# Query and key rows of two heads rounded in one step and moved to their tiles by transfers on chip, with a new order of the queues

## The chip, the cores and the metric

The kernel runs on one core of a Trainium2 chip. The metric is device time in microseconds (us) of one execution. Engines are called as in the profile: PE (TensorE), with its weight loads as PEld, DVE (VectorE), ACT (ScalarE), POOL (GpSimd) and SP (SyncE), of which the last here only issues transfers (DMAs) from memory.

## What is computed

The reference is one decoder block for 512 tokens of width 1024: a recurrent branch (RG-LRU) and a branch of latent attention with 16 heads, merged by gates, then a convolved feed-forward part (FFN). The change lies in the attention branch. Cut to what matters:

```python
q = (rmsnorm(q_lat, q_norm_g[l]) @ w_uq[l]).reshape(B, S, H, QK_NOPE + QK_ROPE)   # 64 + 32
q_rope = rotary(q[..., QK_NOPE:], positions)
q = jnp.concatenate([q[..., :QK_NOPE], q_rope], axis=-1)
kv = (rmsnorm(kv_lat, kv_norm_g[l]) @ w_ukv[l]).reshape(B, S, H, QK_NOPE + V_HEAD)
k_nope, v = kv[..., :QK_NOPE], kv[..., QK_NOPE:]
k_r = jnp.broadcast_to(rotary(k_rope, positions)[:, :, None, :], (B, S, H, QK_ROPE))
k = jnp.concatenate([k_nope, k_r], axis=-1)
y_mla = causal_block_attention(q, k, v)
```

## The kernel before

Activations lie transposed: features on the 128 partitions, the 512 tokens along the row. Every matmul is done in float32r with each operand split into a rounded high part and the low rest (three matmuls instead of one, mm3, L255). A split is therefore always a pair: ACT rounds a copy (the high part), DVE subtracts it from the source (the low part). Weights are loaded by SP into "raw" buffers (L242) and split into "whl" or "whg" (L221 and L222).

The order in time is: latents and modulation of the first norm (0 to 60 us), attention (60 to 240), the recurrence (240 to 380), the two output projections (to 460), the norm and the FFN (to the end). In between stand matmuls of the gates ("fill", L544) and sums for the second modulation (L781 on DVE), which are independent of the attention and are put where something is waited for.

For the attention the 16 heads form four groups g. A head's query tile "q" and key tile "kt" have 96 rows in use: 64 without rotation ("nope") and 32 rotated ("rope"). q_nope(g, i), L671, projects the nope rows of two heads i at once: one 128x512 result in the PSUM bank "fil", rows 0 to 63 of the first head and 64 to 127 of the second. evac_half (L666) then splits 64 rows at a time straight into rows 0 to 63 of each head's tile: L668 on ACT and L669 on DVE, twice. k_nope(g, i), L688, does the same for two key tiles. There is one bank "fil"; the next projection into it waits until both halves have been read. q_rope(g), L679, rotates the rope rows of four heads in one tile "rp" (of which one buffer exists), and q_rope_put (L684) brings each head's 32 rows to rows 64 to 95 of its query tile by a DMA on chip, issued by POOL (L686). head_a (L715) computes scores (L725 to L727: high by high, high by low, low by high), softmax, and transposes the probabilities (L747); head_b (L753) multiplies by the values (L760).

The order in which each engine does its instructions up to the FFN is written out by hand: QUEUES (L103) has for each engine a table of numbers in base 36, the places that instructions have in the order of the code, and queue_order (called at L1068) chains them in the order of the table. So the order does not follow from the code alone.

Of the kernel before, what the change touches and what calls it, by code (L numbers as in the profile page):

```python
# [98 lines left out]
GACC = ()  # L99
ROOM = -1  # L100
# [4 lines left out]
        0-7 b 8 c 9 d a e-u w-x 1h-1i v 10 13 y 1j 16 19 1c z 1k 11 14 12 15 17-18 1a-1b 1d-1g 1l-21 26 29 2c 22  # L105
        2n-2q 27-28 2a 23 2b 24-25 2d-2h 38-3b 2i-2m 2r-37 3c-3f 3t 3g 3u-3v 3h 3w 3i-3s 3x 40 43 46 3y 41 44 47
        49-4a 3z 42 45 48 4b 4e 4h 4k 4n 4f 4i 4l 4c-4d 4o 4q-4r 4g 4j 4m 4p 4s-4v 5j-6i 7s-7t 6j 7u-80 6k-6u 7j-7q
        81-89 4w-53 7r 54-58 6v-6z 59 70 5a 8m 71 5b 72 8n-8r 5c 73 5d 74 91 94 9a 5e 75 9b 95-99 92-93 8s-90 9c 5f
        76-78 5g-5i 79-7h 9n-9y 7i ba bd-bk 9z-aa 9d 9h 9l 9i-9k 9e-9g 9m bb-bc bl aj-ao 8a-8c ab-ad cp cs cy ae-af
        8d-8h cz ct-cv bm bq-bt bn-bp cw-cx cq-cr d0 ag ap-ax bu-bv ea ed ej-ek ee-ei bw-bz eb-ec el ah-ai 8i-8l  # L110
        ay-b1 c4-cc d1-d4 c0-c3 d5-d8 b2-b4 dj-do b5 d9-da b6-b9 db-df cd-ch em-ep ci dp-ds eq-et dt-dx eu-ev dg-di
        fg fj-fq ew cj-cl ex fh ey-ez fi fr g2-gd hp-hs hy-hz ht-hx ge-gp i0 f0-f1 fs fw-fy f2 fz f3 ft-fv cm-co
        dy-e9 g0 gq gy-h3 gr-gt g1 f4-f6 j4 j7 jd gu j8-jb i1-i4 jc je j5-j6 jf i5-i8 h4-h5 i9-ia h6-ha ib-ie hb-hc
        if gv-gx kp ks ky-kz kt-kx ig-ii kq-kr l0 f7-fa ij-ir fb jg jk-jn jh-jj jo-jp fc-fd jy-k3 fe-ff hd-hg jq-js
        l1-l4 jt-ju hh-hn l5-la jv-jx ho k4-kc lb-li is-iu lj lm ls-lt ln-lr lk-ll lu iv-iw m5-m7 ng m8 nh-ni ix
        nj-nr m9-mg iy-j3 kd-ke mh-ms kf-kh lv-lz m3 m0-m2 m4 ki n1-n6 mt-n0 ns nw-nz nt-nv p7 pa-pf o0-o1 p8-p9
        n7-nf kj-kl pg r4-r6 km-ko ph-pi r7-ra oj-ol rd-re om rb on rc rf oo-op oa-oi oq-ox q1-q6 oy-p6 o2 pj-pm
        o3-o9 pn-pq sa sd sj-sk se-si pr-ps q7-qf ua-uc pt rg-rn pu-q0 sb-sc sl qg-qj ro-rp qk-ql sw qm sx-sy ud-ul
        sz rq t0-t7 rr-rx qn-qo sm-st qp t8-tj qq-qx ts-tx su-sv qy-r0 vg vj vp r1-r2 vk-vo vh-vi vq-vr r3 tk um
        uq-ut un wa-wc uo-up tl wd-wl tm uu-uv tn-tp uw-uz tq-tr ry v0 rz-s0 v1-v3 s1 vs-vv s2-s9 ty vw-vz tz w0-w1  # L120
        u0-u9 w2 wm-wp w3 wq-wt w4-w9 v4-v6 wu-wv v7-v8 ww-wy 104-107 v9 wz-x0 va x1-x2 vb x3 vc-vf x4-x7 xg-xh x8
        xi-xn x9 xo xa xp-xr xb-xe xs-xt xf xu-z6 108-109 z7-z8 10a-10t zg 10u zh 10v zi-zo 112-113 zp-zq 114-11d zr
        z9 10w 10y 110 10x 10z 111 11e-11p zs-101 11w-11x 102-103 11y-127 za-zd 128-129 ze-zf 12a-12j 11q-11r 11t
        11s 11u-11v 12q-136 13e-13f 137 13g-13p 148-149 12k-12l 12n 12m 12o-12p 14a-14c 13q-13r 14d-14f 13s-141
# [1397 lines left out]
```

## Time and profile before

| | us |
|---|---|
| median of 3 runs | 845.07 |
| lowest and highest of them | 843.25, 846.47 |
| the profiled execution | 844.61 |
| its span, first to last instruction | 842.8 |
| PE busy | 827.0 |
| DVE busy | 744.3 |
| ACT busy | 542.0 |
| POOL busy | 23.9 |

A row of the profile names the line of the code, the engine, the operation and the tiles (out<-in, without buffer numbers). In a table of groups there follow the shapes and the count, after the first bar the busy time in us and the mean ns of one, after the second bar the engine's idle time just before them and who ended it. In a timeline a row has the start in us and the time it took, and in brackets the idle time before it with its releaser. Matmuls overlap in PE's pipeline: one of 512 columns is shown with 0.4 us, but they start 0.23 us apart.

### The profile page before, as it was taken

How to read it: one execution, taken by the hardware profiler on the slowest of the kernel's cores; microseconds unless marked ns; L12 is line 12 of the kernel's file. 1: busy time of each engine (PE TensorE's matmuls, PEld its weight loads, DVE VectorE, ACT ScalarE, POOL GpSimd, SP SyncE). 2: the span in 40 equal slices, each digit the busy share in tenths (PEclk: the TensorE clock that was granted, in tenths of full speed). 3: DMA queues.
4: the chain of work that ended last, by engine and by line, in shares of the span. 5: the costliest groups of instructions: out<-in, count | busy, mean ns of one | idle time of the engine just before them, and what ended most of it. 6: DMA issues, size and time to landing. Idle time of an engine off the chain costs nothing. (4 is left out here: it accounts for less than half of the span.)

```text
span 842.8 us, 12809 instructions
## 1 busy us (share of the span) xinstructions
PE 827.0 (98%) x4612; PEld 697.8 (83%) x4612; DVE 744.3 (88%) x1440; ACT 542.0 (64%) x1032; POOL 23.9 (3%) x47
## 2 busy tenths in 40 slices
PE   7999999999999999999999999999999999999996
PEld 4777888888877777777877898899889889889985
DVE  7989898998957899998689769999999999999985
ACT  7585877777846888893145567676666666545533
POOL 0001000000020000000000001000000000000000
PEclk9999999999999999999999999999999999999999
DMA  9923233344573232227665155332232233522222
GB/s 348 376 93 86 85 104 125 103 151 119 173 177 96 75 111 87 97 89 276 210 234 192 74 187 137 88 115 94 93 115 95 90 117 135 194 73 101 103 99 100
DMA packets 35107, 114.15 MB, mean 135 GB/s; under 512 B 4434, under 2 KB 8146, under 8 KB 34532
## 3 DMA queue, kind: packets, MB, share of 16 engines
q1 hardware_dynamic: 32548, 107.01, 36.3%
q0 software_dynamic: 2496, 6.33, 3.7%
q8 instruction: 36, 0.59, 0.3%
q14 instruction: 27, 0.22, 0.1%
HBM read 106.47 MB, written 4.23 MB: 131 GB/s over the span
## 5 line engine op out<-in xcount | busy, mean ns | idle before, releaser
L221 ACT ACTIVATE whl<-raw 128x512 fp32r<-128x512 f32 (+2 forms) x149 | 84.4, 573 | 71.0 <-PE tr L260 25.4
L221 ACT ACTIVATE whg<-raw 128x512 fp32r<-128x512 f32 x136 | 84.6, 625 | 43.1 <-PE acc L260 9.8
L222 DVE TENSOR_TENSOR whg<-raw,whg 128x512 fp32r<-128x512 f32 x136 | 92.5, 686 | 14.0 <-ACT whg L221 13.2
L222 DVE TENSOR_TENSOR whl<-raw,whl 128x512 fp32r<-128x512 f32 (+2 forms) x149 | 91.3, 619 | 10.0 <-ACT whl L221 9.3
L737 ACT ACTIVATE P<-P,mx,qsc 128x512 f32<-128x512 f32 (+3 forms) x64 | 41.2, 647 | 7.7 <-DVE mx L733 7.7
L1199 DVE SCALAR_TENSOR_TENSOR Y<-acc,vec,Y 128x511 f32<-128x511 f32 (+1 forms) x38 | 28.2, 745 | 9.0 <-ACT Y L1197 8.8
L1199 DVE SCALAR_TENSOR_TENSOR Y<-Y,vec 128x511 f32<-128x511 f32 (+1 forms) x48 | 35.3, 746 | 0.4
L258 PE MATMUL gm<-A,whg 128*128 128x512 f32 x88 | 35.4, 402 | 0.0
L260 PE MATMUL gm<-A,whg 128*128 128x512 f32 x88 | 35.4, 402 | 0.0
L259 PE MATMUL gm<-A,whg 128*128 128x512 f32 x88 | 35.2, 400 | 0.0
L258 PE MATMUL tr<-A,whl 128*128 128x512 f32 x80 | 32.1, 402 | 0.0
L258 PE MATMUL acc<-A,whg 128*128 128x512 f32 x80 | 31.8, 397 | 0.0
L260 PE MATMUL tr<-A,whl 128*128 128x512 f32 x80 | 31.7, 397 | 0.0
L259 PE MATMUL tr<-A,whl 128*128 128x512 f32 x80 | 31.7, 396 | 0.0
L260 PE MATMUL acc<-A,whg 128*128 128x512 f32 x80 | 31.7, 396 | 0.0
L259 PE MATMUL acc<-A,whg 128*128 128x512 f32 x80 | 31.6, 395 | 0.0
L730 DVE CUSTOM_DVE_ANT_0 P<-acc,mr 128x256 f32<-128x256 f32 (+2 forms) x64 | 28.6, 486 | 2.1 <-PE acc L727 1.7
L221 ACT ACTIVATE pt<-tr 128x512 fp32r<-128x512 f32 (+1 forms) x48 | 23.5, 520 | 8.4 <-PE tr L747 6.5
L222 DVE TENSOR_TENSOR pt<-tr,pt 128x512 fp32r<-128x512 f32 (+1 forms) x48 | 27.6, 594 | 0.2
L760 PE MATMUL tr<-pt,v 128*128 128x384 f32 (+3 forms) x128 | 27.7, 324 | 0.0
L260 PE MATMUL acc<-A,whl 128*128 128x512 f32 x64 | 25.7, 401 | 0.0
L259 PE MATMUL acc<-A,whl 128*128 128x512 f32 x64 | 25.3, 395 | 0.0
(601 smaller groups left out, 2572.6 us busy)
## 6 DMA issues: line engine op xcount, KB each, us to landing
raw<-in_w_up SPq DMA_DIRECT2D x44, 512.0 KB, 3.5
raw<-in_w_dn SPq DMA_DIRECT2D x22, 512.0 KB, 3.5
wa<-in_w_adat SPq DMA_DIRECT2D x16, 512.0 KB, 9.5
raw<-in_w_adat SPq DMA_DIRECT2D x16, 512.0 KB, 3.3
raw<-in_w_xr SPq DMA_DIRECT2D x10, 512.0 KB, 3.5
raw<-in_w_pr SPq DMA_DIRECT2D x10, 512.0 KB, 4.1
raw<-in_w_gm SPq DMA_DIRECT2D x8, 512.0 KB, 4.2
raw<-in_w_gr SPq DMA_DIRECT2D x8, 512.0 KB, 3.5
```

The lines of the kernel that those rows point to most:

```text
L221: S.activation(h, src, AF.Copy)
L222: return V.tensor_tensor(dst[:, 1, lo_c:lo_c + n], src, h.bitcast(F32), SUB).ins
L258: PE.matmul(out, wh, x[:, 0, xs], start=start, stop=False)
L259: PE.matmul(out, wh, x[:, 1, xs], start=False, stop=False)
L260: return PE.matmul(out, wl, x[:, 0, xs], start=False, stop=stop).ins
L730: V.tensor_tensor_reduce(out=pt[:, POFF[qd]:POFF[qd] + n], in0=sc[qd], in1=mask[:, T - n:], scale=1.0, scalar=-3e38, op0=ADD, op1=ALU.max, ...
L737: S.activation(pq, pq, AF.Exp, scale=qsc[:, qb:qb + 1], bias=mx[:, qb:qb + 1], accum_out=sm[:, qb:qb + 1])
L760: PE.matmul(yb[:, kb * P:], vv, pth[:, part, off:off + n], start=(i == 0 and part == 0), stop=(i == 3 and part == 1))
L1199: V.scalar_tensor_tensor(u[:, d:], src[:, :T - d], vc("fw", (2 - d) * 2 * NF + cj), u[:, d:], MUL, ADD)
```

## The change

Three things are changed.

First, the query rows. The weight columns of w_q are swapped on the host, so that the second head of a pair comes out in rows 0 to 63 and the first in rows 64 to 127. The new evac splits all 128 rows in one pair of steps into the second head's tile. The first head's rows, which then lie in rows 64 to 127 of the wrong tile, are brought to rows 0 to 63 of their own tile by a DMA on POOL's queue (move). The put of the second head's rope rows writes rows 64 to 95 of the tile from which that move reads.

Second, the key rows. They are split on 128 rows into the buffer "rp", and two moves bring them to the two key tiles. As "rp" has one buffer, k_nope(g, 0) now stands behind q_rope_put(g, 1) in the code.

Third, the tables of QUEUES are new for all five engines. Of the tables SP's first line is shown; its new first entry is the load of the positions.

```diff
+QMOVE = tuple(range(8))
+KMOVE = tuple(range(8))
...
     "SP": """
-        0 2-a c b d-m o-p n r 1 s u q t w-y v z 1b 10-1a 1c-25 37 26-36 38 3t 39 3o-3p 3a-3b 3q-3r 3c-3n 3s 3w 3z
+        u 0 2-a c b d-m o-p n r q s 1 t w-y v z 1b 10-1a 1c-26 37 27-36 3o-3p 3t 38-39 3q-3r 3a-3n 3s 3w 3z 3u-3v 3x
...
+        def evac(dst, psrc):
+
+            S.activation(dst[:, 0, :], psrc, AF.Copy)
+            V.tensor_tensor(dst[:, 1, :], psrc, dst[:, 0, :].bitcast(F32), SUB)
+
+        def move(dst, src, half):
+
+            put(dst[0:64].bitcast(F32), src[64 * half:64 * half + 64].bitcast(F32))
+
         def q_nope(g, i):
             b = bank("fil")
             project(b, wq[g], i, 3, lambda k: qn[k], ahead=AHQ)
+
+            ts = [hl(p1, "q", QB) for _ in range(2)]
             for j in range(2):
-                t = hl(p1, "q", QB)
-                qt[4 * g + 2 * i + j] = t
-                evac_half(t, b[64 * j:64 * j + 64, :])
+                qt[4 * g + 2 * i + j] = ts[j]
+            if 2 * g + i in QMOVE:
+                evac(ts[1], b)
+                move(ts[0], ts[1], 1)
...
         def k_nope(g, i):
             b = bank("fil")
             project(b, wkv[g], i, 2, lambda k: kvn[k], ahead=AHQ)
-            for j in range(2):
-                evac_half(kt[(4 * g + 2 * i + j) % KT], b[64 * j:64 * j + 64, :])
+            ts = [kt[(4 * g + 2 * i + j) % KT] for j in range(2)]
+            if 2 * g + i in KMOVE:
+                w = hl(p1, "rp", 1)
+                evac(w, b)
+                for j in range(2):
+                    move(ts[j], w, j)
...
         fill()
-        k_nope(0, 0)
         q_nope(0, 1)
         q_rope_put(0, 1)
+        k_nope(0, 0)
...
                 if i == 2:
-                    k_nope(g + 1, 0)
                     q_nope(g + 1, 1)
                     q_rope_put(g + 1, 1)
+                    k_nope(g + 1, 0)
...
-        n0 = b[:, :, 0:2, :NOPE].reshape(3, P, P)
-        n1 = b[:, :, 2:4, :NOPE].reshape(3, P, P)
+        n0 = b[:, :, 1::-1, :NOPE].reshape(3, P, P)
+        n1 = b[:, :, 3:1:-1, :NOPE].reshape(3, P, P)
```

In the changed file the same statements stand 1 to 23 lines lower (L222 becomes L223, L575 L576, L686 L702, L781 L804, L968 L991), and buffer numbers differ a little.

Three places show what the new order does. The first is POOL's queue for the third group of heads (g = 2); L686 is a rope put, and what follows is the clearing of a later accumulator. Before:

```order
L686 DMA q_1191<-rp_1067 32x1024
L686 DMA q_1644<-rp_1528 32x1024
L686 DMA q_1424<-rp_1528 32x1024
L686 DMA q_1427<-rp_1528 32x1024
L686 DMA q_1647<-rp_1528 32x1024
L567 MEMSET acc_2760 128x1024
```

Now, with L679 for a move and L702 for a rope put, from the two key moves of the group before it:

```order
L679 DMA kt_715<-rp_1404 64x1024
L679 DMA kt_716<-rp_1404 64x1024
L679 DMA q_1424<-q_1425 64x1024
L702 DMA q_1425<-rp_1527 32x1024
L702 DMA q_1424<-rp_1527 32x1024
L679 DMA q_1627<-q_1628 64x1024
L702 DMA q_1627<-rp_1527 32x1024
L702 DMA q_1628<-rp_1527 32x1024
L679 DMA kt_713<-rp_1646 64x1024
L679 DMA kt_714<-rp_1646 64x1024
```

Four puts in a row have become two moves with two puts behind each, and the key moves stand behind all of them. The put into q_1425 waits for the move out of it, and the moves out of rp_1646 come from a rounding into "rp" that waits for the puts out of rp_1527.

The second place is DVE late in the attention, around the split of the probabilities (pt_2170 before, pt_2169 now) for the transposes of the next head; L781 (now L804) is a sum for the second modulation on a freshly loaded weight. Before:

```order
L222 TENSOR_TENSOR pt_2043<-tr_2042,pt_2043 128x256
L765 TENSOR_TENSOR Y_503<-Y_503,tr_1922 64x512
L669 TENSOR_TENSOR q_2090<-fil_2075,q_2090 64x512
L781 ISA raw_2212,B_501<-raw_2212,crow_1091,vec_82 128x1024
L781 ISA B_501 128x1
L222 TENSOR_TENSOR pt_2170<-tr_2169,pt_2170 128x512
```

Now:

```order
L223 TENSOR_TENSOR pt_2042<-tr_2041,pt_2042 128x256
L756 TENSOR_TENSOR mx_2138<-mx_2138,nqsc_695 128x4
L804 ISA raw_2211,B_501<-raw_2211,crow_1090,vec_82 128x1024
L804 ISA B_501 128x1
L788 TENSOR_TENSOR Y_503<-Y_503,tr_1921 64x512
L788 TENSOR_TENSOR Y_503<-Y_503,tr_2047 64x512
L223 TENSOR_TENSOR whl_2266<-raw_2264,whl_2266 128x256
L223 TENSOR_TENSOR pt_2161<-tr_2160,pt_2161 128x512
L223 TENSOR_TENSOR pt_2169<-tr_2168,pt_2169 128x512
```

The sum still stands ahead of that split, with four other steps between them now.

The third place is DVE in the output projection: whl_4279 and whg_4298 are splits of a weight of w_out, and L575 (now L576) adds a weight's rows into mr for the second gate. Before:

```order
L222 TENSOR_TENSOR whg_4258<-raw_4237,whg_4258 128x512
L575 SCALAR_TENSOR_TENSOR mr<-R_4273,cact,mr 128x512 x2
L575 SCALAR_TENSOR_TENSOR mr<-R_4294,cact,mr 128x512 x2
L575 SCALAR_TENSOR_TENSOR mr<-R_4313,cact,mr 128x512 x2
L968 TENSOR_TENSOR R_2678<-R_2678,T_499 128x512
L222 TENSOR_TENSOR whl_4279<-raw_4277,whl_4279 128x512
L222 TENSOR_TENSOR whg_4298<-raw_4277,whg_4298 128x512
```

Now:

```order
L223 TENSOR_TENSOR whg_4258<-raw_4237,whg_4258 128x512
L991 TENSOR_TENSOR R_2678<-R_2678,T_499 128x512
L576 SCALAR_TENSOR_TENSOR mr<-R_4254,cact,mr 128x512 x2
L223 TENSOR_TENSOR yhl_4161<-R_2678,yhl_4161 128x512
L576 SCALAR_TENSOR_TENSOR mr<-R_4273,cact,mr 128x512 x2
L576 SCALAR_TENSOR_TENSOR mr<-R_4294,cact,mr 128x512
L223 TENSOR_TENSOR whl_4279<-raw_4277,whl_4279 128x512
L223 TENSOR_TENSOR whg_4298<-raw_4277,whg_4298 128x512
```

Of the six additions from R_4273 to R_4313, three now stand behind the two splits; the two with R_4254, which stood ahead of this piece, have moved into it.

More of the change, by code (lines that the diff above doesn't have):

```diff
@@ L104 @@
     "PE": """
[L105 to L124, printed above, removed]
@@ new lines @@
+        0-7 b 8 c 9 d a e-u w-x 1h-1i v 10 13 y 1j 16 19 1c z 1k 11 14 12 15 22-25 17-18 1a-1b 1d-1g 1l-1s 2n-2q
+        1t-21 26 29 2c 27-28 2a-2b 2d-2h 38-3b 2i-2m 2r-2z 3t 30 3u 31 3v 32 3w 33-37 3c-3s 3x 40 43 46 3y 41 44 47
+        49-4a 3z 42 45 48 4b 4e 4h 4k 4n 4f 4i 4l 4c-4d 4o 4q-4r 4g 4j 4m 4p 4s-4v 5j-6d 7s 6e 7j-7q 7t 6f-6g 7u 6h
+        7v 6i 7w-7y 6j 7z-80 6k-6u 4w-54 81-89 55-5c 8m-8u 5d-5e 7r 5f-5i 6v-7i 8v-90 8a-8g 9n-9w 8h 9x-9y 8i-8l
+        ay-b0 9z 91-94 9a-9b 95 a0 96 a1 97 a2 98 a3-a4 99 9c a5-aa ba bd-bh bj-bk bi bb-bc aj-ao bl b1-b3 9d-9h 9l
@@ new lines @@
+        9i-9k 9m b4-b5 ap-ax ab-ad b6 ae-ai b7-b9 cp-cs cy-cz ct-cx d0 ea-ec c4-c8 ed-ei c9 ej-el ca-cc bm bq-bu
+        bn-bp bv cd-cf dj-dq bw dr cg bx-bz d1-d4 c0 ch-cj ds-dt ck-co dy d5-d8 dz-e1 du d9-da c1-c3 dv db-df em-ep
+        dg-dh eq-et di dw-dx e2-e3 eu-ev e4-e5 ew-ez e6 f0 e7-e9 f1-f3 g2-gd f4-fa fg fj-fo fh-fi fp-fr ge hp-i0
+        gf-gp fb-fe fs fw-g0 ft-fv g1 ff hd-he gy-h3 gq-gx hf-hh h4-hc i1-i5 i9 i6-i7 j4-j7 jd-je j8-jb ij-il kp-kr
+        jc jf im-io i8 ia ks-kv ky-kz kw-kx l0 ip-ir ib-ie hi-hj jg-jn jy-k6 hk if hl-ho ig-ii jo jq k7-kc jr-jt jp
@@ L673, in q_nope @@
             project(b, wq[g], i, 3, lambda k: qn[k], ahead=AHQ)
+            ts = [hl(p1, "q", QB) for _ in range(2)]
             for j in range(2):
-                t = hl(p1, "q", QB)
-                qt[4 * g + 2 * i + j] = t
-                evac_half(t, b[64 * j:64 * j + 64, :])
+                qt[4 * g + 2 * i + j] = ts[j]
+            if 2 * g + i in QMOVE:
+                evac(ts[1], b)
+                move(ts[0], ts[1], 1)
+            else:
+                for j in range(2):
+                    evac_half(ts[j], b[64 - 64 * j:128 - 64 * j, :])
         def q_rope(g):
@@ L690, in k_nope @@
             project(b, wkv[g], i, 2, lambda k: kvn[k], ahead=AHQ)
-            for j in range(2):
-                evac_half(kt[(4 * g + 2 * i + j) % KT], b[64 * j:64 * j + 64, :])
+            ts = [kt[(4 * g + 2 * i + j) % KT] for j in range(2)]
+            if 2 * g + i in KMOVE:
+                w = hl(p1, "rp", 1)
+                evac(w, b)
+                for j in range(2):
+                    move(ts[j], w, j)
+            else:
+                for j in range(2):
+                    evac_half(ts[j], b[64 * j:64 * j + 64, :])
         def v_group(g):
```

107 lines of the change are left out of this document (58 added, 49 removed).

## The prediction

> **What bounds the kernel now.** The first view is the page's busy time, then the table of windows by stage, then the timeline of TensorE at each place where it stood still. On the page TensorE is busy in nearly the whole span:
>
> ```profile
> span 842.8 us, 12809 instructions
> ...
> PE 827.0 (98%) x4612; PEld 697.8 (83%) x4612; DVE 744.3 (88%) x1440; ACT 542.0 (64%) x1032; POOL 23.9 (3%) x47
> ```
>
> By stages (us, then busy us of PE, weight loads, DVE, ACT, POOL; granted clock, DMA share, GB/s), the start, attention, recurrence, projection and the rest:
>
> ```profile
> 0.00:20.00 20.00, 15.18 (x37) 8.06 (x38) 14.19 (x36) 14.67 (x25) 1.63 (x10) 0.91 0.91 344
> 20.00:60.00 40.00, 40.00 (x186) 31.42 (x185) 38.11 (x79) 27.27 (x42) 0.00 (x0) 1.00 0.63 241
> 60.00:240.00 180.00, 179.12 (x1003) 151.65 (x1002) 158.75 (x409) 130.65 (x304) 12.43 (x24) 1.00 0.37 118
> 240.00:380.00 140.00, 140.00 (x615) 106.69 (x614) 120.59 (x189) 110.16 (x171) 4.57 (x8) 1.00 0.35 108
> 380.00:460.00 80.00, 78.24 (x334) 61.55 (x333) 66.84 (x107) 29.33 (x55) 0.00 (x0) 1.00 0.69 236
> ```
>
> The rows of heads are rounded between 60 and 240 us. There PE is busy 179.12 of 180 us, and DVE 158.75. So DVE and ACT have room, PE has none, and work taken from DVE or ACT is worth only what PE waits for them. Those waits can be counted. A matmul of 512 columns follows the one before it by 0.23 us (444.88 to 445.11 below); three starts between 20 and 460 us come about 1 us late:
>
> ```profile
> 201.76 0.40 PE L258 MATMUL gm<-A,whg 128*128 128x512 f32 x1
> 202.91 0.44 PE L747 MATMUL tr<-ident,P 128*128 128x128 f32 x2 [0.76 <-DVE pt L222]
> ...
> 381.23 0.39 PE L260 MATMUL fil<-yhl,whg 128*128 128x512 f32 x1
> 382.46 0.50 PE L258 MATMUL tr<-yz,whg 128*128 128x512 f32 x1 [0.84 <-ACT whg L221]
> ...
> 444.88 0.40 PE L858 MATMUL gm<-whg,yhl 128*128 128x512 f32 x1
> 445.11 0.40 PE L856 MATMUL gm<-whl,yhl 128*128 128x512 f32 x1
> 446.40 0.50 PE L857 MATMUL acc<-whl,yhl 128*128 128x512 f32 x1 [0.89 <-DVE whl L222]
> ```
>
> Start to start less 0.23 they cost 0.92, 1.00 and 1.06, together 2.98 us. The order of TensorE is the same in both programs in the second half, and the count and shapes of its matmuls are the same throughout. So the change can win these 3 us and little else, and whatever it makes TensorE wait for is lost one for one.
>
> **The rounding itself.** It removes 32 roundings and 32 subtractions on 64 rows, and adds 16 and 16 on 128 rows. Mean ns stands behind the second bar:
>
> ```profile
> L221 ACT ACTIVATE pt<-tr 128x512 fp32r<-128x512 f32 x32 | 18.1, 592 | 5.8 <-PE tr L747 5.7
> ...
> L668 ACT ACTIVATE kt<-fil 64x512 fp32r<-64x512 f32 x16 | 9.5, 592 | 4.9 <-PE fil L260 3.3 <-DVE kt L669 1.4
> L668 ACT ACTIVATE q<-fil 64x512 fp32r<-64x512 f32 x16 | 9.5, 592 | 10.3 <-PE fil L260 10.0 <-DVE q L669 0.2
> ...
> L222 DVE TENSOR_TENSOR pt<-tr,pt 128x512 fp32r<-128x512 f32 x32 | 21.6, 685 | 0.1
> ...
> L669 DVE TENSOR_TENSOR q<-fil,q 64x512 fp32r<-64x512 f32 x16 | 11.0, 687 | 1.3 <-ACT q L668 1.0
> L669 DVE TENSOR_TENSOR kt<-fil,kt 64x512 fp32r<-64x512 f32 x16 | 11.0, 687 | 1.2 <-ACT kt L668 0.9
> ```
>
> 128 rows take as long as 64 (592 against 592 ns, 685 against 687). ACT is spared 16 x 0.592 = 9.5 us and DVE 16 x 0.687 = 11.0 us. Both lie beside the 179 us of matmuls and are worth nothing by themselves. The bank "fil" also comes free about one pair (0.6 us) earlier; TensorE had other work there.
>
> **The moves.** 24 transfers of 256 KB (64 rows) are added to POOL's queue: one for each of 8 query steps, two for each of 8 key steps. Before, that queue carried the rope puts, 128 KB on 32 rows, and later eight transfers of 256 KB on 64 rows:
>
> ```profile
> L686 POOL DMA_DIRECT2D q<-rp x16: 489/489/497, 72.3 to 193.0; - x16
> ...
> DMA to landing us min/median/max: 2.1/3.1/6.8
> ...
> L926 POOL DMA_DIRECT2D yr<-rd x8: 594/610/624, 238.9 to 243.0; - x8
> ...
> DMA to landing us min/median/max: 3.9/6.2/8.7
> ```
>
> Issuing costs POOL 0.49 us each, 24 x 0.49 = 12 us on an engine that was busy 12.43 of 180. No row shows a 64-row move on chip. The fastest put of half the bytes landed after 2.1, the slowest after 6.8. The eight large ones landed (243.0 + 8.7 - 238.9 - 3.9) / 7 = 1.27 us apart, so the further 128 KB are worth some 0.65, and I take 2.8 us, bounds 2.1 and 6.8. The Trainium skill, SBUF — State Buffer, section "Door 1: The DMA port swizzle", speaks against such a move: 64 neighbouring rows reach no more ports than 32, so the rate is about 218 GB/s and half the chip's. The 1.27 us for 256 KB (206 GB/s) agree. With that page's fixed 2 us its estimate would be 3.2 us, and the sum below would be 1.6 us higher (0.4 at each of four heads).
>
> Where does that latency lie on the path? A key move goes from the last matmul of its projection (0.40) over ACT (0.59), DVE (0.69) and landing (2.8) to the first score matmul: 4.5 us. Before, only 1.7 of it were needed. The new order of TensorE gives it work meanwhile. Between projection and first score stand 28, 28, 28 and 29 matmuls for heads 0, 6, 10 and 14 (counted from 0), and more for all others. The tightest is head 10: 12 of 512 columns, 3 of 384, 3 of 128 and 10 transposes.
>
> ```profile
> 198.68 1.03 PE L747 MATMUL tr<-ident,P 128*128 128x128 f32 x8
> 199.47 1.23 PE L760 MATMUL tr<-pt,v 128*128 128x512 f32 x7
> ```
>
> Eight transposes fill 0.79 us, 0.1 each, so head 10 has 12 x 0.23 + 3 x 0.17 + 3 x 0.06 + 10 x 0.1 = 4.4, and 0.23 of the last projection matmul itself: 4.7 us against 4.5 (0.17 and 0.06 by width). That just fits. I put 0.2 us of new wait on each of the four heads, 0.8 in all; bounds are 0 (landing 2.1) and about 3.8 each (landing 6.8). The second key move is half a microsecond behind, but its head comes one head later.
>
> Two waits are added beside this. The put into the second head's rows 64 to 95 must wait until the move has read them, and holds POOL's queue for those 2.8 us; next in that queue is the next query move. And the buffer "rp", of which there is one, now also takes the keys, so a key step rounds only after the rope puts of its group have landed. k_nope(g, 0) therefore goes behind q_nope(g, 1). That chain (move 2.8, put up to 3.1, after 1.7 of matmul, ACT and DVE) is 7.6 us after the query projection. In groups 2 and 3 the key projection comes before it has ended, but then 72 and 63 matmuls stand ahead of the score (at 180 / 1003 = 0.18 us each 13 and 11 us), which hide it. Uncovered, either would cost some 4 us.
>
> **The order.** The positions' DMA moves from 29th to first of SP's queue, and their conversion to first of DVE's:
>
> ```profile
> 0.74 0.39 SPq L296 DMA_DIRECT2D vec<-in_vec  x1
> 1.19 1.84 SPq L339 DMA_DIRECT2D T<-in_x  x4
> ...
> posi<-in_pos SPq DMA_DIRECT2D x1, 256.0 KB, 9.6
> ...
> 6.18 1.23 DVE L363 CUSTOM_DVE_ANT_0 junk<-T 128x1024 f32<-128x1024 f32 x1 [1.75 <-DMA T<-in_x]
> ...
> 10.63 1.28 DVE L454 CUSTOM_DVE_ANT_0 wa<-wa,crow,vec 128x1024 f32<-128x1024 f32 x1 [0.92 <-DMA wa<-in_w_adat]
> ...
> 15.24 1.65 PE L508 MATMUL acc<-A,wls 128*128 128x512 f32 x3 [0.88 <-ACT A L484]
> ```
>
> The start waits for DMA, first for x, then for w_ada. Everything behind is issued 1.19 - 0.74 = 0.45 us later, and 256 KB at 344 GB/s are 0.74 us of transfer. So the first projection at 15.24 comes 0.45 to 1.2 us later; I take 0.5, since data only begin to flow after the issue and most of the transfer falls into that lead. DVE's two extra steps on the path are covered by the 0.92 idle at 10.63. Nothing comes back at 27.8, where the DMA stood: PE is busy 40.00 of 40 us there.
>
> The wait at 446.40 goes: its split now stands behind three additions into mr fewer (4.07 us / 6 = 0.68 each, 2.0 us), more than 1.06:
>
> ```profile
> 441.07 4.07 DVE L575 SCALAR_TENSOR_TENSOR mr<-R,cact,mr 128x512 f32<-128x512 f32 x6 [1.24 <-DMA R<-in_w_ada]
> 445.06 0.68 DVE L968 TENSOR_TENSOR R<-R,T 128x512 f32<-128x512 f32 x1
> 445.66 0.68 DVE L222 TENSOR_TENSOR whl<-raw,whl 128x512 fp32r<-128x512 f32 x1
> ```
>
> The one at 202.91 is DVE waiting for a slow weight load ahead of the split that TensorE needs:
>
> ```profile
> 200.96 1.28 DVE L781 CUSTOM_DVE_ANT_0 raw<-raw,crow,vec 128x1024 f32<-128x1024 f32 x1 [1.73 <-DMA raw<-in_w_adat]
> ...
> 202.17 0.68 DVE L222 TENSOR_TENSOR pt<-tr,pt 128x512 fp32r<-128x512 f32 x1
> ```
>
> In the new order four other steps stand between the two, but the load is still ahead, so I count 0.64 of 0.92. At 382.46 the weights' rounding moves as its neighbours do; I count half, 0.5. Sum of what goes: 1.06 + 0.64 + 0.5 = 2.2 us, bounds 0 and 2.98.
>
> **Sum.** The profiled execution took 844.61 us, 0.46 under the median of 845.07. 844.61 + 0.5 - 2.2 + 0.8 = 843.7, on the median's footing 844.2 us.
>
> **Rivals.**
> - *Everything hides* (0.15): all three waits go and no move is late: 844.61 + 0.5 - 2.98 + 0.46 = 842.6 us. For it speaks that the new order left room exactly where "rp" is late; against it the pile-up at 200 us, where transfers came late.
> - *The new order brings nothing* (0.20): the three waits stay, being DMA and buffers: 844.61 + 0.5 + 0.8 + 0.46 = 846.4 us.
> - *Late moves*, the slower side (0.14): the wait for a DMA takes the place of the wait for DVE. Were the moves to land 2.0 us later than I take, as puts did in the pile-up (up to 6.8), four heads would wait 1.8 us more: 843.7 + 7.2 - 0.8 + 0.46 = 850.6 us. It decides from a landing of about 4.5 us on, where each of the four waits 1.5. Against it: the median of the puts is 3.1.
> - *Faster by over 0.5%* (0.06): no wait in the trace pays for it; it would need closer matmuls or a shorter start.
>
> **Chances and range.** My forecast has 0.45. It, the first two rivals and 845.07 itself lie within 0.5%, about what a measurement of this kernel can tell from no change (840.8 to 849.3): 0.80 the same, 0.06 faster, 0.14 slower. The range goes from the first rival less the 1.4 us by which runs of before lie above their median, 841.2, up to 849.5, most of the way to late moves.
>
> **What would show it.** Right: the first projection 0.5 us later, no late start at the places of 202.91 and 446.40, landings of moves near 2.8 us, PE still above 97%, DVE's busy time 11 us lower. Wrong: "DMA q" or "DMA kt" as what ended PE's waits at heads 0, 6, 10 and 14, ACT idle at the key rounding for longer than the matmuls hide, or a start that moves by over 1.2 us.

## The result, and the profile after

The changed kernel took 852.7 us (median of four runs, 851.8 to 854.5) against 844.16 us (842.93 to 846.47) before: ratio 1.0095, 95% interval 1.0079 to 1.0111. It is slower by about 8 us. The forecast was 844.2 with a range up to 849.5, so both the value and the range were missed. (The forecast stood on a median of 845.07; a fourth run of before brought it to 844.16.) The profiled execution took 852.24 us, 7.6 more than that of before. Of all executions timed for this document one, of the kernel "gains" below, took 1348.5 us at a granted clock of 0.557, and is left out of its ratio.

In the changed file the statements stand 1 to 23 lines lower than before: splits L222 (ACT) and L223 (DVE), the new 128-row split L674 and L675, the moves L679, scores L748 to L750. In the kernels of the experiments they stand up to four lines off that. The page of the changed kernel:

```profile
span 850.5 us, 12813 instructions
...
PE 829.4 (98%) x4612; PEld 697.2 (82%) x4612; DVE 733.1 (86%) x1424; ACT 532.6 (63%) x1016; POOL 36.2 (4%) x71
```

DVE has 11.2 us less to do, ACT 9.4 less, POOL 12.3 more, as forecast; the number of matmul records is the same. Still the span is 7.7 us longer. The table by stage (us, then busy us of PE, weight loads, DVE, ACT, POOL; granted clock, DMA share, GB/s):

```profile
60.00:240.00 180.00, 177.45 (x981) 149.39 (x980) 144.92 (x388) 119.04 (x284) 23.20 (x45) 1.00 0.52 153
...
380.00:460.00 80.00, 76.93 (x325) 59.88 (x325) 62.66 (x97) 28.06 (x48) 0.43 (x1) 1.00 0.64 218
```

DVE's relief is there (144.92 against 158.75 in attention), and PE has lost busy time in the same stage (177.45 against 179.12). PE's waits, added up by line and releaser (us in all, times, longest):

```profile
PE acc L748 <- DMA kt<-rp: 2.5, 2, 1.9
...
PE tr L259 <- ACT whl L222: 1.8, 1, 1.8
...
PE gm L879 <- DVE T L1013: 0.7, 1, 0.7
```

The waits of before at 202.91 and 446.40 are gone from this list. In their place stand waits for the moved keys, for a split of weights, and for a sum on DVE. How far the changed kernel is behind at one and the same amount of TensorE work shows where the time went. For it each matmul counts 0.231, 0.175, 0.118 or 0.061 us by its 512, 384, 256 or 128 columns, and the two profiled executions are read where the sums are equal. (A transpose counts 0.061 by this and takes 0.1, so in the attention some tenths can come from the order alone.)

| time in before, us | 34 | 76 | 98 | 142 | 185 | 231 | 311 | 392 | 412 | 454 | 474 | 820 |
|---|---|---|---|---|---|---|---|---|---|---|---|---|
| changed kernel behind by, us | 1.3 | 0.8 | 2.9 | 3.2 | 4.7 | 2.6 | 3.4 | 4.4 | 7.3 | 6.7 | 7.9 | 7.6 |

Three steps up matter: 2.1 at 90 us, 1.5 between 142 and 185, 2.9 at 396. There is one large step down, 2.1 at about 203, of which the wait of before explains 0.9; the other 1.2, and 0.7 of the step between 142 and 185, are not explained here. Behind 474 little changes any more.

**The late keys.** Scores of head 0 on TensorE and the pair of moves for them in POOL's queue, then the scores of head 10:

```profile
86.95 1.02 POOL L679 DMA_DIRECT2D kt<-rp  x2 [4.06 <-DVE rp L675]
...
90.07 0.32 PE L728 MATMUL fil<-whl,kvn 128*128 128x256 f32 x1
92.33 0.36 PE L748 MATMUL acc<-kt,q 96*128 96x256 f32 x1 [1.94 <-DMA kt<-rp]
```

```profile
179.72 0.82 PE L770 MATMUL tr<-ident,P 128*128 128x128 f32 x6
181.14 0.39 PE L748 MATMUL acc<-kt,q 96*128 96x256 f32 x1 [0.60 <-DMA kt<-rp]
```

From the issue at 86.95 to the end of the cover (90.07 and 0.12) are 3.2 us. A landing of 2.8 would have fitted; head 0's first key landed after 5.3. At head 10 six transposes fill 0.6 from 179.72, so the score is 0.8 late. The view of the new lines gives durations of issue in ns, and the landing of all 24 moves:

```profile
L679 POOL DMA_DIRECT2D kt<-rp x16: 509/512/519, 87.0 to 222.1; - x16
...
DMA to landing us min/median/max: 2.8/3.7/5.4
```

2.8, the forecast for all of them, was the fastest. The rate in the Trainium skill, SBUF — State Buffer, "Door 1: The DMA port swizzle", with the fixed 2 us of the same page's "The DMA setup-cost knee", gave the estimate of 3.2, nearer to the median of 3.7 but far from head 0's 5.3.

**The weights of the projection.** Of before, a load of w_pr and ACT's split of it:

```profile
384.96 0.33 SPq L242 DMA_DIRECT2D raw<-in_w_pr  x1
...
390.09 0.63 ACT L221 ACTIVATE whl<-raw 128x512 fp32r<-128x512 f32 x1 [5.08 <-DMA raw<-in_w_pr]
```

The same in the changed kernel, with SP's queue ahead of it and TensorE behind it:

```profile
387.78 1.00 SPq L1003 DMA_DIRECT2D Y<-in_x  x2
...
389.59 0.33 SPq L243 DMA_DIRECT2D raw<-in_w_pr  x1
...
396.94 0.39 PE L259 MATMUL tr<-yr,whl 128*128 128x512 f32 x1
398.44 0.63 ACT L222 ACTIVATE whl<-raw 128x512 fp32r<-128x512 f32 x1 [4.35 <-DMA raw<-in_w_pr]
399.12 0.50 PE L259 MATMUL tr<-yr,whl 128*128 128x512 f32 x1 [1.78 <-ACT whl L222]
...
401.11 0.50 PE L261 MATMUL tr<-yr,whl 128*128 128x512 f32 x1 [0.51 <-DVE whl L223]
```

Two loads of x now stand ahead of this weight in SP's queue. It is issued at the same point of the work (4.6 us later, with a lag of 4.4), but ACT has it 8.85 us after the issue instead of 5.13. TensorE, start to start less 0.23, waits 1.95 and 0.67.

**Smaller things.** A run of six matmuls on 64 rows is cut in two by the new order of TensorE, and each half takes as long as a whole one:

```profile
349.86 0.96 PE L911 MATMUL acc<-xh,whl 64*128 64x512 f32 x3
350.75 0.50 PE L259 MATMUL fil<-yhl,whg 128*128 128x512 f32 x1
355.58 0.97 PE L911 MATMUL acc<-xh,whl 64*128 64x512 f32 x6
356.48 0.50 PE L261 MATMUL fil<-yhl,whg 128*128 128x512 f32 x1
```

Three take 0.89 us, six take 0.90. The six start in pairs (355.58, 355.92 and 356.15), one of each pair on rows 0 to 63 and one on rows 64 to 127; in the three that were left together all are on the same rows, and they start one by one. So cutting the run undid the pairs. And most of what is won at 446 is given back at 466, to another step of DVE:

```profile
465.88 0.39 PE L881 MATMUL fil<-yr,yhl 128*128 128x512 f32 x1
466.93 0.50 PE L879 MATMUL gm<-yr,yhl 128*128 128x512 f32 x1 [0.66 <-DVE T L1013]
```

### The profile page after: what moved, and what is told of

Read it like the earlier page. It is cut to its first block, busy times and chain, and to the rows that moved or that the text cites. A ratio compares the mean times of both kernels' runs of the same rounds, so it can differ in the third digit from the quotient of the medians.

```text
span 850.5 us, 12813 instructions
## 1 busy us (share of the span) xinstructions
PE 829.4 (98%) x4612; PEld 697.2 (82%) x4612; DVE 733.1 (86%) x1424; ACT 532.6 (63%) x1016; POOL 36.2 (4%) x71
## 4 chain that ended last, share of the span: by engine, by line
PE 75%; DVE 12%; DMA 5%; ACT 4%; issue 3%; POOL 0%; ACTq 0%; DVEq 0%; SPq 0%; POOLq 0%
PE acc L261 4%; PE acc L259 4%; PE acc L260 4%; PE acc L1167 4%; PE tr L259 4%; PE tr L261 4%; PE tr L260 4%; PE gm L260 3%; PE gm L259 3%; PE gm L261 3%; PE tr L1167 3%; PE fil L261 2%; PE fil L259 2%; PE fil L260 2%; PE tr L783 2%
## 5 line engine op out<-in xcount | busy, mean ns | idle before, releaser
L222 ACT ACTIVATE whl<-raw 128x512 fp32r<-128x512 f32 (+2 forms) x149 | 84.1, 574 | 83.9 <-PE tr L261 30.6
L222 ACT ACTIVATE whg<-raw 128x512 fp32r<-128x512 f32 x136 | 84.4, 625 | 43.5 <-DVE raw L1182 9.2
L223 DVE TENSOR_TENSOR whg<-raw,whg 128x512 fp32r<-128x512 f32 x136 | 92.4, 685 | 11.9 <-ACT whg L222 11.6
L223 DVE TENSOR_TENSOR whl<-raw,whl 128x512 fp32r<-128x512 f32 (+2 forms) x149 | 91.1, 618 | 12.0 <-ACT whl L222 11.3
L760 ACT ACTIVATE P<-P,mx,qsc 128x512 f32<-128x512 f32 (+1 forms) x64 | 41.1, 646 | 11.5 <-DVE mx L756 11.4
L753 DVE CUSTOM_DVE_ANT_0 P<-acc,mr 128x256 f32<-128x256 f32 (+3 forms) x64 | 28.7, 486 | 8.8 <-PE acc L750 8.7
L223 DVE TENSOR_TENSOR pt<-tr,pt 128x512 fp32r<-128x512 f32 (+1 forms) x48 | 27.5, 596 | 5.8 <-ACT pt L222 5.6
L222 ACT ACTIVATE pt<-tr 128x512 fp32r<-128x512 f32 (+1 forms) x48 | 23.4, 520 | 10.4 <-PE tr L770 9.9
L261 PE MATMUL acc<-A,whl 128*128 128x512 f32 x64 | 25.7, 401 | 0.0
L783 PEld LDWEIGHTS tr<-pt,v 128*128 128x128 f32 x128 | 21.6, 188 | 4.8 <-DVE pt L223 1.3
```

The costliest lines, as they stand in the source:

```text
L222: S.activation(h, src, AF.Copy)
L223: return V.tensor_tensor(dst[:, 1, lo_c:lo_c + n], src, h.bitcast(F32), SUB).ins
L261: return PE.matmul(out, wl, x[:, 0, xs], start=False, stop=stop).ins
L753: V.tensor_tensor_reduce(out=pt[:, POFF[qd]:POFF[qd] + n], in0=sc[qd], in1=mask[:, T - n:], scale=1.0, scalar=-3e38, op0=ADD, op1=ALU.max, ...
L760: S.activation(pq, pq, AF.Exp, scale=qsc[:, qb:qb + 1], bias=mx[:, qb:qb + 1], accum_out=sm[:, qb:qb + 1])
L783: PE.matmul(yb[:, kb * P:], vv, pth[:, part, off:off + n], start=(i == 0 and part == 0), stop=(i == 3 and part == 1))
```

## The experiments

The theory after the result: the rounding and the moves are not dear by themselves; the time went to the keys that land late, to the weight behind the two loads, and to small losses of the new order. The rivals: the positions' load at the start, the new order as a whole, or moves whose traffic slows everything. Edits of a table are given as what moved. Each ratio is against runs of the kernel before that were made beside it (medians 844.77 to 845.59).

### The start

The first kernel puts the positions' load and DVE's conversion of them back; the second only the conversion.

```diff
 SP:  -u 0 2-a ... r q s 1          +0 2-a ... r q s u 1
 DVE: -1u 0 1v 1-3 ... 1f 1w        +0 1-3 ... 1f 1u-1w
```

> The changed kernel, with the positions' load and their conversion on DVE put back to their old places in the two queues, and nothing else. Theory A (the new order of the queues costs some 5 us, late key moves 3): the 256 KB load in front of the small load of vec made vec land at 5.30 instead of 2.46 us, and the first projection start at 17.30 instead of 15.24; 1.0 us of that came back, since TensorE kept its full clock there. So the first projection is at 15.2 to 15.4 again, TensorE's clock falls to 0.5 there again, and the whole is 1.0 to 1.3 us faster than the changed kernel, some 851.5. Theory B (the 24 moves on chip slow everything by their traffic, the order is innocent): no more than my predicted 0.5 us, some 852.2.

> The changed kernel, with only DVE's conversion of the positions put back to its old place; their load stays first in SP's queue. If the load in front of the small one is what delays the start, vec still lands at about 5.3 us, the first projection stays at about 17.3, and nothing is won (852.7). If DVE waiting for the positions at the head of its queue is the cause, the first projection goes back to 15.3 and the time falls by 1.0 to 1.3 us.

Measured: 852.48 us, ratio 1.0083 (1.0063 to 1.0102), and 852.02, ratio 1.008 (1.0065 to 1.0095). Nothing is won by either. Yet the load does delay the start. In the changed kernel the small load of vec stands behind it:

```profile
0.74 0.39 SPq L403 DMA_DIRECT2D posi<-in_pos  x1
1.18 0.42 SPq L297 DMA_DIRECT2D vec<-in_vec  x1
...
5.33 0.21 ACT L312 ACTIVATE cact<-vec 128x8 f32<-128x8 f32 x1 [3.31 <-DMA vec<-in_vec]
...
17.30 0.96 PE L509 MATMUL acc<-A,wls 128*128 128x512 f32 x3 [0.76 <-ACT A L485]
```

With the load put back, ACT has vec at 2.42 and the first projection starts at 15.40, 1.9 us earlier:

```profile
2.42 0.21 ACT L311 ACTIVATE cact<-vec 128x8 f32<-128x8 f32 x1 [0.40 <-DMA vec<-in_vec]
...
13.68 1.02 PE L480 MATMUL tr<-ident,T 128*128 128x128 f32 x4 [1.54 <-ACT T L379]
15.40 1.65 PE L508 MATMUL acc<-A,wls 128*128 128x512 f32 x3 [0.70 <-ACT A L484]
```

With the conversion alone put back, ACT has vec at 5.08 and the first projection starts at 16.88, so most of the delay is the load's.

The gain is lost to the clock. The windows from 16 to 17 us, first with the load put back, then of the changed kernel (the third number from the end is the granted clock):

```profile
16.00:17.00 1.00, 1.00 (x4) 0.80 (x3) 1.00 (x3) 1.00 (x3) 0.00 (x0) 0.50 1.03 391
```

```profile
16.00:17.00 1.00, 0.55 (x5) 0.30 (x3) 1.00 (x3) 0.61 (x2) 0.00 (x0) 1.00 1.02 399
```

Behind the wait of 1.54 us at 13.68 the clock is halved. In the changed kernel TensorE has no such gap there, and its later projections run at full clock. To test that, a third kernel fills the gap of the kernel before with three matmuls that are used for nothing:

```diff
+for _ in range(3):
+    PE.matmul(wb, ones, mask, start=True, stop=True)
```

> The kernel before, with three more matmuls on ones whose result nobody reads, two of them between the transposes of the first and of the second half of x (TensorE idle for 1.53 us there) and one behind these (0.88 us idle). In every profile with the old start the granted clock falls to 0.5 behind these gaps for 4 to 7 us, at 14 to 20 us; in those with the changed start, which left no such gap, it doesn't. If the gap is the cause, the clock stays at 1.0, the first projection's matmuls follow by 0.23 instead of 0.43 us, and the time falls by 2.0 to 3.0 us, to some 842.3: this is what made the changed start cost less than the 2.1 us by which its first projection is late. If not, it stays at 844.8.

Its window:

```profile
16.00:17.00 1.00, 0.96 (x5) 0.43 (x3) 1.00 (x3) 1.00 (x3) 0.00 (x0) 1.00 1.06 405
```

The clock is 1.00 now, where the profile of before has 0.50 from 15 to 18 us, so the gap was the cause of its fall. The time does not change: 845.53 us, ratio 1.0001 (0.9993 to 1.001). Two things eat the gain. The three matmuls are 1.4 us of work by the count above, so that at equal work of the rest this profile is only 0.4 us ahead of before at 76 us, and 0.7 at 700. And then it loses 1.3 us to two waits for a split of a weight that the profile of before does not have:

```profile
708.21 0.50 PE L1145 MATMUL tr<-T,whl 128*128 128x256 f32 x2 [0.30 <-ACT whl L220]
709.35 0.86 PE L1145 MATMUL tr<-T,whl 128*128 128x256 f32 x5 [0.64 <-DVE whl L221]
```

So in time the start is as good as neutral, both ways.

### The projection's weight

First the two loads of x go behind the two weights. Then, as well, DVE's two splits of the weight go ahead of the sum that stood right before them.

```diff
 SP:  -3q-3r ... 3a-3b              +3a-3b 3q-3r
 DVE (second kernel alone): h4 (a sum of the modulation) goes behind h0 (the second split)
```

> The changed kernel, with one exchange in SP's queue: the two loads of the residual into Y that stand ahead of the next weights for the gates and w_pr (387.78 and 388.46 us) go behind them, as they stood before. Theory A: the load of w_pr issued at 389.59 took 8.8 us instead of 5.1, because 1 MB for Y was ahead of it; TensorE waited 1.9 us at 396.94 and 0.7 at 400.21 for that weight. With the exchange it lands after about 5, both waits go, and the time falls by 2.4 to 2.9 us, to some 850. Rival: the splits on DVE, moved behind the scans, free the buffer late, and the weight comes late whatever stands in the queue: no gain, 852.7.

> The changed kernel with the exchange of the loads of the run before (the two loads into Y behind the next weights), and on DVE the addition for the second modulation that waited 3.01 us for its own load set behind the two splits of the weight of w_pr. In the run with the exchange alone that weight landed at 396.3 instead of 398.1, but its split on DVE came at 400.86 all the same. Theory A': DVE's queue, held by an addition whose load is late, was what came last. With both edits TensorE waits no longer than 0.3 us at 397 to 400, and the time falls by 2.0 to 2.6 us, to some 850. Rival: something else is late next, such as the residual's loads, and the time stays at 852.5.

With the loads alone nothing is won: 854.09 us, ratio 1.011 (1.0091 to 1.0129). The weight comes in time, and ACT has split it at 397. But DVE does its instructions in order, and stands at a sum whose own weight now comes late:

```profile
396.38 0.63 ACT L221 ACTIVATE whl<-raw 128x512 fp32r<-128x512 f32 x1 [1.25 <-DMA raw<-in_w_pr]
...
400.19 0.75 DVE L575 SCALAR_TENSOR_TENSOR acc<-raw,cact,acc 128x512 f32<-128x512 f32 x1 [3.01 <-DMA raw<-in_w_ada]
400.86 0.68 DVE L222 TENSOR_TENSOR whl<-raw,whl 128x512 fp32r<-128x512 f32 x1
```

With both edits: 850.78 us, ratio 1.0064 (1.0046 to 1.0081, just touching that of the changed kernel). DVE's split stands ahead of the slow weight, and TensorE has no wait left at this place:

```profile
396.92 0.68 DVE L222 TENSOR_TENSOR whl<-raw,whl 128x512 fp32r<-128x512 f32 x1
...
399.29 1.41 DVE L575 SCALAR_TENSOR_TENSOR acc<-raw,cact,acc 128x512 f32<-128x512 f32 x2 [1.08 <-DMA raw<-in_w_ada]
```

The step of 2.9 us at 396 is gone from the lag: 5.3 at 392 us, 5.3 at 412, and 5.4 at the end, where the changed kernel has 7.6. The cause at this place is shown: the weight behind the two loads, and in DVE's queue its split behind a sum that waits for another load.

### The split run of gate matmuls

```diff
 PE:  18l 18n 18p go behind 18o, so that the run of six is whole again
```

> The changed kernel, with the six gate matmuls on 64 rows joined again to one run of six on TensorE, which the new table had split into three at 339.54 and three at 349.86 us. Theory A: a run of six takes 0.90 us, and each run of three takes 0.90 too, so the split costs 0.9 us: 851.8. Theory B: nothing changes, 852.7.

851.58 us, ratio 1.0076 (1.0062 to 1.009). In the trace the runs are of six again, and the place is 0.5 us shorter, not 0.9. The interval overlaps that of the changed kernel, so the times alone do not show it.

### The moves, and the order without them

Here key pair 0 is rounded by halves again, straight into its tiles; then all sixteen pairs are, in the order of the changed kernel.

```diff
-KMOVE = tuple(range(8))
+KMOVE = tuple(range(1, 8))     # first kernel
+QMOVE = KMOVE = ()             # second kernel
```

> The changed kernel, with the first two heads' keys split on 64 rows straight into their tiles as before (one rounding and one subtraction more, two moves less); all other moves and the order stay. Theory A: TensorE waits 1.8 to 2.4 us for head 0's moved keys at 90 us, and in three of five profiles its granted clock then falls to 0.5 for 3 to 6.5 us, which costs 1.5 to 3.2 us more. Both go: 2.1 us and on the mean some 1.5 us, from 852.5 to some 849. Theory B (the moves' traffic slows everything): two of 24 moves less win 0.3 us.

> The changed kernel without any move: all query and key rows are split on 64 rows straight into their tiles, as before, in the changed order of the queues. Theory A: beside the wait at head 0 with its fall of the clock (some 3.6 us on the mean) that at head 10 goes too (0.6 to 1.1); the rest is the order's: 847.5 to 848.5. Theory B: the order is innocent, so the time is that of before or less, 843 to 845.5.

With one pair by halves: 850.31 us, ratio 1.0059 (1.0045 to 1.0073). The wait at 92 is gone, and another comes, for the bank "fil":

```profile
86.24 0.40 PE L258 MATMUL gm<-A,whg 128*128 128x512 f32 x1
87.86 0.36 PE L727 MATMUL fil<-whl,kvn 128*128 128x256 f32 x1 [1.22 <-DVE kt L669]
```

The forecast said that TensorE had other work while "fil" is read, which held for the order of before. In the new order it has none there. With all pairs by halves the kernel takes 869.15 us, ratio 1.029 (1.0269 to 1.031), where 847.5 to 848.5 was expected. TensorE now waits at sixteen places of the attention, 0.5 to 1.7 us at each and 20 us together. At eight of them, as at 87.86 above, the half that DVE splits last holds "fil"; at the others TensorE waits for other steps of DVE and ACT, whose queues now have 16 steps more each.

So the rival that the new order as a whole is bad without regard to the moves is not the whole of it: order and 128-row rounding belong together. In that order the rounding is worth some 16 us (869.15 less 852.7).

In the order of before, the converse: four of the eight query pairs are rounded on 128 rows, and the keys stay in halves.

```diff
+QMOVE = (0, 3, 5, 7)
+KMOVE = ()
```

> The kernel before in its own order, with four of the eight query steps (0, 3, 5 and 7) split on 128 rows and the first head's rows moved on chip; the key rows and the other query steps stay on 64 rows. ACT and DVE have 2.4 and 2.8 us less to do, POOL issues 4 moves. The query moves have 8 to 16 us of TensorE's work ahead of the first scores, and landed after 2.8 to 3.7 us in the changed kernel. Theory A: nothing changes, 845.5, since neither the rounding nor the move is on the path. Theory B (traffic of the moves): 1 us slower. Rival C (less work on DVE and ACT is worth something in the old order too): over 1 us faster.

843.85 us, ratio 0.9989 (0.9978 to 1.0000): no change that can be told. So four moves slow nothing that the times show. TensorE waits once more, 0.65 us before a score at 79.06, for a rope put: POOL could issue the puts only from 75.10 on, after the move issued at 71.75 had landed, and in before it issues them from 72.27. This is the put behind a move that the prediction describes. The remaining pairs and the keys were not tried in the old order; for the keys a queue would there wait for "rp" behind a step that waits for that queue.

### Where the keys' latency comes from

Head 0's two moves are issued within 0.5 us of each other. If they slowed each other, a gap between them would bring the first one in sooner. Nine memsets on POOL, 3.3 us, make that gap at every pair; the second kernel does the same to the mended kernel (below).

```diff
-for j in range(2):
-    move(ts[j], w, j)
+move(ts[0], w, 0)
+for _ in range(9):
+    G.memset(gap, 0.0)
+move(ts[1], w, 1)
```

> The changed kernel, with nine small clearings of an unused tile (2.7 us of POOL) between the two key moves of each pair, so that the second starts when the first should have landed. In the changed kernel the two are issued 0.5 us apart and the first lands after 5.29 us at head 0 and after 3.1 to 4.0 at the others, where query moves that go alone land after 2.8 to 3.7. Theory A (two moves at once share the transfer engines, which is what my 2.8 us left out): the first key move lands after some 2.9 everywhere, the waits at heads 0 (2.1 us) and 10 (0.8) go, with them the fall of the clock, and the time goes from 852 to some 848.5. Rival: the weights' loads that are issued beside them (85.77 and 87.02 us) hold the engines, so the first move still lands after more than 4.5 us at head 0, and nothing is won.

> The kernel with all repairs (848.55) and the same space between the two key moves. If late keys are what is left of the loss there (1.4 and 0.7 us at head 0, 1.0 at head 10, 0.7 to 0.8 at heads 6 and 14 in some executions), it falls to 845.5 to 846, one us above before. If something else is left, it stays at 848.5.

```profile
86.26 0.51 POOL L679 DMA_DIRECT2D kt<-rp  x1 [3.90 <-DVE rp L675]
86.77 3.29 POOL L713 MEMSET gap<- 128x256 f32 x9
```

```profile
91.36 0.36 PE L750 MATMUL acc<-kt,q 96*128 96x256 f32 x1 [1.63 <-DMA kt<-rp]
```

Alone in flight the first key still lands after 5.0 us, so the second move is not the main cause. The times, 867.38 (ratio 1.0252, 1.0226 to 1.0278) and 861.9 (1.0207, 1.0187 to 1.0227), come from the second heads, which now wait for the later move (2.3 to 4.5 us at the worst three). What else was in flight at head 0 shows in the changed kernel's transfers from 86 to 93 us:

```profile
q8 instruction: 1, 0.02, 1.4%
...
kt<-rp POOLq DMA_DIRECT2D x2, 256.0 KB, 5.3
raw<-in_w_q SPq DMA_DIRECT2D x2, 192.0 KB, 2.4
```

One packet that loads instructions holds one of the 16 DMA engines for 1.6 us (1.4% of 16 x 7 us), and two weight loads run beside. Over the nine profiles with both moves at once the landing of the first grows with the time of that packet, from 4.96 us at 0.89 to 5.87 at 2.21, 0.6 to 0.7 us per us. The two with the gap (5.01 at 2.02, 4.58 at 1.37) lie some 0.65 below that line: so much may be the second move. For the rest this is a correlation and no more; neither the packet nor the loads were taken away, since the rotating buffers fix the order of those loads.

### More cover at head 0

```diff
 PE:  a0-aa (matmuls of the values' projection) go behind 9z, ahead of head 0's scores
 ACT: 2f ahead of 2h    DVE: 3x ahead of 3m
```

> The changed kernel, with nothing of its work changed: on TensorE eleven matmuls of the values' projection, which stood behind the first scores, go ahead of them (1.3 us), and the split of their result goes forward on ACT and DVE. If head 0's keys are simply late (moves that land after 5.3 us behind too little cover), TensorE's wait at 90 us falls from 1.8 to 2.4 to some 0.9 us, its clock does not fall behind it, and the time goes from 852.5 to some 850.3 (1.3 us, and some 1 us on the mean for the clock). If the wait is of another kind (the matmuls ahead make the transfers later, or the work is missed behind the scores), it comes back at 97 to 100 us and nothing is won.

851.63 us, ratio 1.0077 (1.0064 to 1.009). The cover is 1.3 us longer, but the key landed after 5.87 us in this profile instead of 5.29, so the wait at head 0 falls only from 2.15 to 1.39 us, and 0.7 comes back at 95 behind a step of head 0's softmax. The matmuls that are put ahead are missing later.

### The tail in the old order

Up to 247 us this kernel is in the changed order, and from there in that of before.

> The changed kernel, with its order and its moves up to 247 us; what is issued after that stands in the order of before, on all queues. Theory A: this takes away the split run of gate matmuls (0.9), the late weight of w_pr (1.8 to 2.9), the wait at 466 for DVE (0.8 to 1.2), and gives back the wait at 446 (1.0): some 3.5 us faster than the changed kernel, 849. The start and the late key moves stay. Theory B: no more than 0.5 us, since the moves are all there.

858.48 us, ratio 1.0159 (1.0141 to 1.0176). The seam itself costs more than was to be found: TensorE waits 7.2 us at 254.86 for a weight's split on DVE, and then runs at half clock to 266.

Behind the seam the lag falls by 0.7 (14.5 at 311 us, 13.8 at the end), where the changed kernel's grows by 4.2 (3.4 to 7.6). That agrees with the losses at 340 to 478 us being those of the new order; as a measurement of time it is spoilt by the seam.

### All mends together, and the gains alone

The mended kernel joins the edits of the weight, the gates and the cover, and moves one more step of DVE (j6 behind ix, for the wait at 466). The other one takes the kernel before and moves only the steps behind the two waits that the new order removed:

```diff
 DVE: 93 8t ahead of 97;  j1 j4 ij behind j3
 ACT: 6t 6k 6e ahead of 74
```

> The changed kernel with all repairs at once: the cover for head 0 (2.2 us), the loads and the addition around the weight of w_pr (2.3, between the 1.7 by times and 2.9 by the trace), the run of six gate matmuls joined (0.9), and the addition that frees the bank gm two steps earlier on DVE at 466 us (0.8). If the loss of 7 us is made of these places, it falls from 852.5 to some 846.3, the time of before within its spread; what is left is head 10's keys (0.6 to 1.1). If the loss is spread over all the kernel by the moves, the sum of the repairs falls short by more than 2 us.

> The kernel before, without any move, in its own order, with two places of the tables changed: at 202 us the split of the probabilities goes ahead of the sum and of the weight that wait for a load, on DVE and on ACT; at 443 us the two splits of the weight of w_out go ahead of one addition of the second modulation on DVE. My prediction counted 0.64 and 1.06 us for these waits. If such gains are real by themselves, the time falls by 1.7 to 2.0 us, from 845.5 to some 843.6. If they are only put off (DVE has no room later), it stays at 845.5.

Mended: 848.55 us, ratio 1.0043 (1.0029 to 1.0057). That is half of the loss, and 2.2 us short of the 846.3 that was expected, which by the expectation's own mark speaks for a loss that is spread over the kernel by the moves. The largest waits that are left in the attention of its trace stand at the heads with late keys (heads 0, 6 and 14 are shown):

```profile
92.01 0.35 PE L746 MATMUL acc<-kt,q 96*128 96x256 f32 x1 [0.78 <-issue]
...
145.51 0.36 PE L746 MATMUL acc<-kt,q 96*128 96x256 f32 x1 [0.57 <-issue]
...
225.88 0.71 PE L746 MATMUL acc<-kt,q 96*128 96x256 f32 x3 [0.50 <-issue]
```

The view names no releaser here, but the moves of these heads landed at 91.92, 145.42 and 225.78, 0.1 us ahead of the scores. Start to start and less the work between, they cost 0.9, 0.8 and 0.7, and head 10 another 1.0: 3.4 us at exactly the four heads that the prediction named, with the sum that had 0.8 for them. Another 0.7 at 94.80 stands behind head 0's softmax, where the matmuls for the cover were taken away. Less the 0.9 of the wait at 202.91 and with 0.5 for the start, 3.7 us remain, and 0.43% of 845 are 3.6. This is a sum of readings from one trace; no run took the late keys away from all four heads.

The gains alone: 844.79 us, ratio 0.9999 (0.9988 to 1.001). In its trace the wait at 202.91 is gone, but two others stand there, 0.5 at 198.45 and 0.6 at 204.06; that at 446 is 0.5 instead of 1.1, and the span is 1.0 us shorter. The times do not show it.

Last, what helped or did not hurt, together in the order of before: the four query moves, the three filling matmuls, and the steps behind the wait at 446.

> The kernel before in its own order, with the four query moves of the run q_alone (843.85), the three matmuls that keep the clock, and the two splits of the weight of w_out ahead of an addition at 443 us. If the gains add up: 843.85 - 2.0 to 3.0 - 0 to 0.5, some 841.3, faster than both kernels. If the clock is not the cause: 843.8.

844.62 us, ratio 0.9996 (0.9988 to 1.0005). Its trace has a wait of 1.0 at 448 again, for ACT's split of that weight, the wait for a rope put as in the kernel with four query moves, and the two waits at 709 and 710 as in the kernel with the filling matmuls. No version was found that beats the kernel before.

## Why the prediction was wrong

**The sum counted what the new order takes away, and not what it brings.** This is the step that failed first: "The order of TensorE is the same in both programs in the second half". It is the same only from about 490 us on. At 340 to 350 a run of gate matmuls is cut (0.9), at 396 a weight stands behind two loads (2.9 with what follows), at 466 a step of DVE is late (0.8). Together some 4.6 us that have no term in the sum. All places named so far (start 0.8, keys 3.0, these 4.6, and 0.2 more than before at 382 to 388, less the waits won at 202.91 and 446.40) add up to some 6.6 of the 7.6 us; the last 1.0 is put down to no place. The weight could have been seen before the result: the diff of SP's line shows 3q-3r, the two loads, ahead of 3a and what follows, where 3a-3b had stood first.

**The landing was mis-sized.** 2.8 us was the fastest of 24; the median was 3.7 and head 0's 5.3. The cover had been worked out rightly: 4.7 us in the forecast for the tightest head, of which 3.0 behind the split, against 3.0 from issue to end of cover at head 10 and 3.2 at head 0. So the place and the mechanism held, and the term of 0.8 should have been 3.0 by the changed kernel's profile (2.15 at head 0, 0.8 at head 10) and 3.4 by that of the mended kernel. The rival "late moves" has this mechanism; its 850.6 counts 1.8 us for each of four heads, and head 0 alone had so much in the changed kernel's profile (2.15; head 10 0.8).

**A term was missing behind the waits: the clock.** In four of eight profiles with a wait of 1.8 to 2.5 us at head 0 the granted clock was halved behind it, in the others it was not. With the positions' load put back, for instance, the wait was 2.2 us:

```profile
92.55 0.40 PE L747 MATMUL acc<-kt,q 96*128 96x256 f32 x1 [2.01 <-DMA kt<-rp]
```

```profile
95.00:96.00 1.00, 1.00 (x5) 1.00 (x6) 0.00 (x0) 0.00 (x0) 0.00 (x0) 0.50 0.00 0
```

The lag grew by 5.1 us there between 76 and 98, against 2.1 in the changed kernel's profile, where the clock stayed at 1.00. The mean granted clock of the four timed executions of the changed kernel agrees: two at 0.997 took 852.24 and 851.8 us, two at 0.995 took 853.16 and 854.5. This also fits that rounding pair 0 by halves wins 0.36% (1.0095 less 1.0059, 3 us), more than the 0.7 us by which the wait is shorter; the intervals of those two lie close together, so the sum is a reading and not a proof.

**The start.** +0.5 was forecast with an upper bound of 1.2 for the first projection; it came 2.06 later (17.30 against 15.24). The cause, vec behind 256 KB, was in the diff's first line and was priced by issue and rate alone. In the end the lag at 76 us is 0.8 in this profile and 0.5 on the mean of the eleven with the new start and the 128-row rounding, but it was also 0.2 to 0.9 in three with the old start. So the right number came with the wrong working.

**The waits that go.** 202.91 and 446.40 went, as forecast (0.92 and 1.06; I had counted 0.64 and 1.06). 382.46 did not: two waits at 386.87 and 387.81 replace it. At 446 the win was given back at 466. And the two wins made alone give nothing that the times show. So the sum's 2.2 for the waits that go was 2.0 by these two, but it counted none of the waits that came in their place.

**Right.** 128 rows take as long as 64, DVE and ACT are spared 11 and 9 us, and in the order of before this is worth nothing: four pairs on 128 rows change nothing. "Worth nothing by themselves" was too wide, though, for the new order. The order that came with the change is built on the shorter reading of "fil", and without it the kernel is 16 us slower still. The query moves, the shared buffer "rp" and POOL's queue cost nothing in the changed kernel, as argued.

What stays open: why a move lands in 2.8 us at one head and in 5.3 at another, why a wait of the same length halves the clock in some executions only, and where the last 1.0 us goes.

## What to carry to other kernels

Where TensorE is busy 98% of the time, a change that spares other engines can only win the few waits that are there, and a new hand-written order brings waits of its own: go through each queue for what now stands ahead of a weight or a split that was just in time, and count that too. For a transfer put between two steps of the path, take the slowest landing of the nearest rows for the first use and not one near the fastest, and ask whether the cover holds for that. A wait is to be mended in all queues at once: with the loads in order, the consumer of another load held the split.
